# FFN up products of a decoder layer: seven half-size block products in place of eight

## The chip, the cores and the metric

The kernel is one launch on one core of a Trainium2 chip. The metric is the device time of one execution in microseconds (us); lower is better. TensorE (PE; PEld is its weight load), VectorE (DVE), ScalarE (ACT), GpSimd (POOL) and SyncE (SP, which issues most loads) each work through their own instruction list in order, and wait for each other through semaphores.

## The reference, cut to what matters

A decoder layer runs on 512 prompt rows and on 32 sample rows (8 sequences of 4), so on 544 rows of width 1024: a mixer of mLSTM and differential attention, cross attention into memory, and at the end a convolutional FFN. Only this last part and the norm ahead of it are touched:

```python
h = rms_norm(x, g_ffn_pre)
u = h @ w_up                                   # 1024 -> 2 * 2752
ext = jnp.concatenate([conv_buf, u], axis=1)
c = b_dw
for j in range(CONV_W):                        # width 3, causal, per feature
    c = c + ext[:, j:j + T] * w_dw[j]
a, g = c[..., :D_FF], c[..., D_FF:]
y = (jax.nn.silu(g) * a) @ w_down              # 2752 -> 1024
x = x + rms_norm(y, g_ffn_post)
```

The first 2752 columns of `w_up` give values, the last 2752 gates. Results must hold float32 accuracy.

## The kernel before, in words

**Accuracy.** Each float32 operand is kept as two tiles, a rounded "hi" part and a "lo" rest (`split`: ACT casts hi, L142; DVE, or POOL where it is named, subtracts to get lo, L143). A product is three matmuls: hi by hi, hi by lo, lo by hi.

**Weights.** `W` is a list of loads in the order of use. There are four slots for split weights. A slot's next content is split when the slot is freed, and its load waits in one of six stage buffers of 1024 columns.

**Rows.** The projection before the FFN (`proj_add`) works in blocks of 128 rows, sample rows first. Its `second` half adds the residual (`ev1`, L1067), and TensorE transposes each block (`norm_turn`, L317) into `fT`: features on partitions, 544 rows on the free axis, in two tiles `q` of four 128-feature steps `k`. The FFN norm's factor for each row is not applied there. `rows_of` computes it (L1079), a small matmul spreads it over all partitions (`spread`, L1459 and L1460), and the up evacuation multiplies by it.

**Up.** The 2752 features are 21 tiles of 128 and a last one of 64, whose value and gate share one tile: 43 up tiles. For each, `gemmB` (L452) runs 8 steps k by 3 matmuls by 2 halves of the rows (256 and 288 columns): 48 matmuls. `Up.ev` takes both halves from PSUM with the row factor (L1486 to L1490) into `u`, and applies the convolution with three DVE operations (L1495 to L1497) into `c`. `gate` takes the silu on ACT (L1503), multiplies on DVE (L1509), and splits the product into `act`. The first four up tiles run half by half (L440), so that they can start before the last row blocks are transposed.

**Groups.** Value and gate of one feature tile are a pair. Pairs go in groups of four; the group [20, 21] stands third. The up products of a group and of the first pair of the next come before the down products of the group (L1584 to L1586, with the sample rows in L366), which are added to `yp` (L1597).

**Order.** The code is written in this order, and the framework's scheduler then fixes one list for each engine. Nothing is reordered at run time.

Of the kernel before, what the change touches and what calls it, by code (L numbers as in the profile page):

```python
# [41 lines left out]
HALF = ((0, 256), (256, ROWS))  # L42

# [30 lines left out]
def kernel(ctx: ExitStack, tc: tile.TileContext, I, O):  # L74
# [15 lines left out]
    npool = ctx.enter_context(tc.tile_pool(name="npool", bufs=5))  # L90
# [94 lines left out]
    warm = cst.tile([P, 512], BF16, name="warm")  # L185
# [93 lines left out]

    def put(xt, q, j0, j1, c0, n, src, eng=None):  # L280
# [29 lines left out]
    def norm_turn(h, n, gname, xt, c0, pool=(True, False)):  # L310

        tmps = []
        for q in range(2):
            ps = at("tp")
            pv = v2(ps, P)[:, :, :n]
            for j in range(4):
                tr(pv[:, j, :], h[:, (4 * q + j) * P:(4 * q + j + 1) * P], ident[:n, :n])  # L317
            tmp = T2([P, 4, n], "ht")
# [10 lines left out]
    class Fill:  # L329
# [5 lines left out]
        def add(self, *gens):  # L335
            self.q.extend(gens)
# [94 lines left out]
    def gemmB(xt, evacs, half_first=False):  # L431

        if half_first:
            slots = [W.get() for _ in evacs]
            for i, (c0, c1) in enumerate(HALF):
# [10 lines left out]
        for ev in evacs:  # L446
# [11 lines left out]
            yield 1.36  # L458

# [505 lines left out]
    csz = cst.tile([P, NB, NS], F32, name="csz")  # L965
# [62 lines left out]
    def proj_add(xt, gname, src, gname2, dst, order=None, scale=None):  # L1028
# [44 lines left out]
        def rows_of(x, n, c0):  # L1073
            if scale is None:
                pend.append((norm_rows(x, n, ACTROWS), n, gname2, target[0], c0, POOLQ))
                return
            pend.append((x, n, gname2, target[0], c0, POOLQ))
            rs = sm.tile([P, 1], F32, name="rsd", tag="rsd", bufs=5)
            VCP(out=rs[:n], in_=rstd(sumsq(x, n, N("hN")[:n]), n, 1, DM))  # L1079
            scale[1].append((rs[:n], c0, n))  # L1080
# [349 lines left out]
    groups = [list(range(g, g + 4)) for g in range(0, 20, 4)]  # L1430
    groups.insert(2, [20, 21])

    def up_slots(js):
        for j in js:
            if j < 21:
# [14 lines left out]
    fT = XT("fT")  # L1450

    rsb = cst.tile([P, ROWS], F32, name="rsb")
    rss = []

    def spread(i):
        while rss and (i or len(rss) > 2):
            rs, c0, n = rss.pop(0)
            ps = at("rsb")
            mm(ps[:, :n], lhsT=rs.broadcast_to([n, P]), rhs=ident[:n, :n], start=True, stop=True)  # L1459
            VCP(out=rsb[:, c0:c0 + n], in_=ps[:, :n])  # L1460

    proj, second = proj_add(oT, "g_mem_post", lambda b: xd[0][rows(b)[0]:rows(b)[0] + rows(b)[1], :], "g_ffn_pre", xd[1],
                            scale=(rsb, rss))
# [8 lines left out]
    class Up:  # L1472


        def __init__(self, ti, cvo):
            self.ti, self.cvo = ti, cvo
# [264 lines left out]
```

## Time and profile before

| | |
|---|---|
| median of 3 runs | 1006.27 us (1004.79 to 1007.79) |
| the profiled execution's own time | 1007.98 us |
| its span | 1006.2 us |
| TensorE busy | 983.6 us (98%) |
| DVE, ACT, POOL busy | 601.6, 386.4, 196.9 us |
| mean granted TensorE clock | 0.989 |
| up matmuls in groups (L452 on fT) | 1872 |

The FFN fills the span from about 587 us on. A row of a group has busy time and mean duration of one behind the first bar, and the engine's idle time ahead of it behind the second. Matmuls are pipelined, so that a record is longer than the distance to the next one; the distance is what counts. The windows view gives each engine's busy time in a stretch.

### The profile page before, as it was taken

How to read it: one execution, taken by the hardware profiler on the slowest of the kernel's cores; microseconds unless marked ns; L12 is line 12 of the kernel's file. 1: busy time of each engine (PE TensorE's matmuls, PEld its weight loads, DVE VectorE, ACT ScalarE, POOL GpSimd, SP SyncE). 2: the span in 40 equal slices, each digit the busy share in tenths (PEclk: the TensorE clock that was granted, in tenths of full speed). 3: DMA queues.
4: the chain of work that ended last, by engine and by line, in shares of the span. 5: the costliest groups of instructions: out<-in, count | busy, mean ns of one | idle time of the engine just before them, and what ended most of it. 6: DMA issues, size and time to landing. Idle time of an engine off the chain costs nothing.

```text
span 1006.2 us, 17149 instructions
## 1 busy us (share of the span) xinstructions
PE 983.6 (98%) x6666; PEld 824.3 (82%) x6666; DVE 601.6 (60%) x1127; ACT 386.4 (38%) x740; POOL 196.9 (20%) x389
## 2 busy tenths in 40 slices
PE   8999999999999999999999999999999999999994
PEld 5999777789765778898667789979987997997983
DVE  6834225642686456743654587836857685675677
ACT  6743322333176547633542443242222222222232
POOL 6610000112232114500000164401101110110115
PEclk9999999999899999999999999999999999999998
DMA  9940224151544267763861673053132314214113
GB/s 305 300 128 22 68 79 129 49 175 35 166 138 128 67 209 229 268 214 130 314 220 38 214 236 106 25 147 84 43 118 67 103 46 126 86 44 131 38 46 110
DMA packets 120402, 130.28 MB, mean 129 GB/s; under 512 B 8423, under 2 KB 85832, under 8 KB 120320
## 3 DMA queue, kind: packets, MB, share of 16 engines
q1 hardware_dynamic: 114136, 125.69, 39.7%
q10 hardware_dynamic: 6184, 3.48, 1.2%
q8 instruction: 53, 0.87, 0.3%
q14 instruction: 29, 0.24, 0.1%
HBM read 112.22 MB, written 16.93 MB: 128 GB/s over the span
## 4 chain that ended last, share of the span: by engine, by line
PE 90%; DMA 3%; DVE 3%; issue 1%; ACT 1%; POOL 1%; SPq 0%; DVEq 0%; POOLq 0%; ACTq 0%
PE mm L452 31%; PE mm L386 7%; PE mm L388 7%; PE mm L387 7%; PE mm L440 6%; PE mm L1584 4%; PE mm L1586 4%; PE mm L1585 4%; PE mm L366 3%; PE sda L1137 2%; PE tpk L1342 1%; PE sca L1293 1%; PE cpo L1323 1%; PE ssc L1352 1%; PE oda L1163 1%
## 5 line engine op out<-in xcount | busy, mean ns | idle before, releaser
L142 ACT CAST wslot<-wst 128x1024 fp32r<-128x1024 f32 (+1 forms) x127 | 131.1, 1036 | 282.0 <-issue 82.5
L452 PE MATMUL mm<-fT,wslot 128*128 128x256 f32 (+1 forms) x1872 | 235.7, 288 | 0.0
L452 PEld LDWEIGHTS mm<-fT,wslot 128*128 128x128 f32 x1872 | 234.7, 188 | 0.7 <-issue 0.4
L143 DVE TENSOR_TENSOR wslot<-wst,wslot 128x1024 fp32r<-128x1024 f32 (+1 forms) x127 | 154.0, 1215 | 117.1 <-ACT wslot L142 117.0
L1584 PE MATMUL mm<-wslot,act 128*128 128x512 f32 (+1 forms) x176 | 70.7, 409 | 0.0
L1585 PE MATMUL mm<-wslot,act 128*128 128x512 f32 (+1 forms) x176 | 69.5, 395 | 0.0
L1586 PE MATMUL mm<-wslot,act 128*128 128x512 f32 (+1 forms) x176 | 69.0, 397 | 0.0
L1491 POOL COPY cvo<-u 128x2 f32<-128x2 f32 x43 | 16.2, 377 | 222.4 <-DVE u L1489 222.4
L386 PE MATMUL mm<-wslot,hT 128*128 128x512 f32 x128 | 52.5, 413 | 0.0
L387 PE MATMUL mm<-wslot,hT 128*128 128x512 f32 x128 | 51.8, 405 | 0.0
L452 PE MATMUL mm<-hT,wslot 128*128 128x288 f32 (+1 forms) x384 | 51.4, 295 | 0.0
L388 PE MATMUL mm<-wslot,hT 128*128 128x512 f32 x128 | 51.1, 402 | 0.0
L452 PEld LDWEIGHTS mm<-hT,wslot 128*128 128x128 f32 x384 | 50.0, 194 | 0.1
L1584 PEld LDWEIGHTS mm<-wslot,act 128*128 128x128 f32 (+1 forms) x176 | 33.1, 189 | 17.7 <-issue 8.6
L1486 DVE TENSOR_TENSOR u<-mm,rsb 128x256 f32<-128x256 f32 x43 | 18.1, 423 | 43.6 <-PE mm L452 43.5
L1586 PEld LDWEIGHTS mm<-wslot,act 128*128 128x128 f32 (+1 forms) x176 | 33.0, 188 | 7.5
L1585 PEld LDWEIGHTS mm<-wslot,act 128*128 128x128 f32 (+1 forms) x176 | 33.1, 188 | 6.5
L1503 ACT ACTIVATE c<-c 128x560 f32<-128x560 f32 x21 | 14.1, 673 | 57.3 <-DVE c L1497 53.8
L1497 DVE SCALAR_TENSOR_TENSOR c<-u,cvT,c 128x560 f32<-128x560 f32 x43 | 34.3, 797 | 0.8
L1496 DVE SCALAR_TENSOR_TENSOR c<-u,cvT,c 128x560 f32<-128x560 f32 x43 | 34.1, 793 | 0.1
L386 PEld LDWEIGHTS mm<-wslot,hT 128*128 128x128 f32 x128 | 24.4, 190 | 10.5 <-issue 5.8
L1597 DVE TENSOR_TENSOR yp<-mm,yp 128x512 f32<-128x512 f32 x40 | 27.3, 689 | 9.5 <-PE mm L1586 9.4
(444 smaller groups left out, 1900.9 us busy)
## 6 DMA issues: line engine op xcount, KB each, us to landing
wst<-in_w_up_dram SPq DMA_DIRECT2D x42, 512.0 KB
wst<-in_w_in_dram SPq DMA_DIRECT2D x28, 512.0 KB
wst<-in_w_down_dram SPq DMA_DIRECT2D x20, 512.0 KB
wst<-in_cache_mem_k_dram SPq DMA_DIRECT2D x16, 512.0 KB
vt<-in_cache_mem_v_dram SPq DMA_DIRECT2D x8, 1024.0 KB
wst<-in_w_mk_dram SPq DMA_DIRECT2D x8, 512.0 KB
xb<-in_x_prompt_dram SPq DMA_DIRECT2D x8, 512.0 KB
wst<-in_cache_dk_dram SPq DMA_DIRECT2D x16, 256.0 KB
```

Source lines behind the costliest of these rows:

```text
L142: nc.scalar.copy(out=hi, in_=src)
L143: (eng or nc.vector).tensor_tensor(out=lo, in0=src, in1=f32(hi), op=SUB)
L386: mm(ps[b], lhsT=xt.hi(k, c0, c0 + n), rhs=s[:, 0, kk, :], start=(k == 0), stop=False)
L387: mm(ps[b], lhsT=xt.hi(k, c0, c0 + n), rhs=s[:, 1, kk, :], start=False, stop=False)
L388: mm(ps[b], lhsT=xt.lo(k, c0, c0 + n), rhs=s[:, 0, kk, :], start=False, stop=(k == nk - 1))
L440: mm(ps, lhsT=s[:, l, k, :], rhs=x(k, c0, c1), start=(k == 0 and j == 0), stop=(k == 7 and j == 2))
L452: mm(ps[i], lhsT=s[:, l, k, :], rhs=x(k, c0, c1), start=(k == 0 and j == 0), stop=(k == 7 and j == 2))
L1496: STT(out=c, in0=u[:, 1:EXT - 1], scalar=w[1], in1=c, op0=MUL, op1=ADD)
L1497: STT(out=c, in0=u[:, 0:EXT - 2], scalar=w[0], in1=c, op0=MUL, op1=ADD)
L1584: mm(ps, lhsT=t[:, 0, c0:c0 + P], rhs=s[:n, 0, i % 2, :], start=st, stop=False)
L1585: mm(ps, lhsT=t[:, 0, c0:c0 + P], rhs=s[:n, 1, i % 2, :], start=False, stop=False)
L1586: mm(ps, lhsT=t[:, 1, c0:c0 + P], rhs=s[:n, 0, i % 2, :], start=False, stop=en)
```

## The change

The 20 full pairs no longer run as two up tiles of 8 steps by 2 halves each. A pair's weights are cut into 2 by 2 blocks (value or gate, first or last 512 features), and the rows into two halves of 272 columns (256 prompt rows and 16 sample rows each). Eight block products of 12 matmuls become seven (Winograd's form of Strassen's scheme), each of 4 steps k by 3 matmuls on 272 columns. The sums that this needs are made in float32 and then split:

- of the rows, once (`Sevenths.sums`): three sums on POOL and one on DVE of 1088 columns each, four splits;
- of the weights, for each pair (`slotsS`): four sums of 512 columns on POOL, in place in the stage buffers, and four slots per pair: the value tile as loaded (`own`), one gate block (`other`, half a slot), and the two tiles after the sums (`sums`);
- of the products (`run`): some accumulate in one PSUM bank; four intermediate results (`p1`, `p4`, `p5`, `u2`) are copied from PSUM by ACT, and four additions on DVE take one bank and one copy into `u`.

Sums over rows need rows that are normed already, so the norm is applied before the transposes (`norm_rows`: sum of squares, factor, ACT multiply), and the factor at the evacuation is gone. `fT` is also kept in float32 (`XE.full`). The convolution's first step goes from DVE to ACT. The tiles 20 and 21, which stay on `gemmB`, come first. The stretch of code that matters:

```diff
+    def slotsS(w, ca, cb):
...
+        def other():
+            sv = tile_of()
+            (a1, a2), (b1, b2) = ((t[:, 0:4], t[:, 4:8]) for t in st)
+            split(sv[:, 0, 0:4], sv[:, 1, 0:4], b2)
+            GTT(out=b2, in0=b1, in1=b2, op=ADD)
+            GTT(out=b1, in0=a1, in1=b1, op=SUB)
+            GTT(out=a1, in0=b2, in1=a1, op=SUB)
+            GTT(out=a2, in0=a2, in1=a1, op=SUB)
+            return sv
...
+        for emit in (own, other, sums(0), sums(1)):
+            W.add(emit)
+
+    class Sevenths:
...
+        def sums(self):
+
+            (x11, x12), (x21, x22) = ((t[:, :, :HR], t[:, :, HR:]) for t in self.xt.full)
+            GTT(out=x11, in0=x12, in1=x11, op=SUB)
+            VTT(out=x12, in0=x22, in1=x12, op=SUB)
+            GTT(out=x22, in0=x22, in1=x11, op=SUB)
+            GTT(out=x21, in0=x21, in1=x22, op=SUB)
+            self.t3 = x12
+            for name, t in (("t4", x21), ("t1", x11), ("t2", x22)):
+                o = self.op[name] = [npool.tile([P, 4, HR], F32R, name="xo", tag="N") for _ in range(2)]
+                split(*o, t)
...
+        def run(self, ua, ub):
...
+            pa, pd, pe, pc = (mmp()[:, :HR] for _ in range(4))
+            s = W.get()
+            self.product(pa, s, 0, ("x", 0, 0))
+            p1 = keep(pa, "p1")
+            self.product(pd, s, 1, ("x", 1, 0))
+            W.free()
+            add(ua, 0, pd, p1)
+            s = W.get()
+            self.product(pe, s, 0, "t4")
+            W.free()
+            p4 = keep(pe, "p4")
+            s, s2 = W.get(), W.get()
+            self.product(pc, s2, 1, "t1")
+            p5 = keep(pc, "p5")
+            self.product(pa, s, 0, "t2", False)
+            u2 = keep(pa, "u2")
+            self.product(pc, s, 1, ("x", 1, 1), False)
+            W.free()
+            add(ua, 1, pc, u2)
+            ua.end()
+            self.product(pa, s2, 0, "t3", False)
+            W.free()
+            add(ub, 1, pa, p5)
+            add(ub, 0, pa, p4)
+            ub.end()
...
         def rows_of(x, n, c0):
-            if scale is None:
-                pend.append((norm_rows(x, n, ACTROWS), n, gname2, target[0], c0, POOLQ))
-                return
...
+            pend.append((norm_rows(x, n, ACTROWS), n, gname2, target[0], c0, POOLQ))
...
-    groups = [list(range(g, g + 4)) for g in range(0, 20, 4)]
-    groups.insert(2, [20, 21])
+    groups = [[20, 21]] + [list(range(g, g + 4)) for g in range(0, 20, 4)]
...
-                VTT(out=u[:, 2:258], in0=ps, in1=rsb[:, 0:256], op=MUL)
...
-            VTS(out=c, in0=u[:, 2:EXT], scalar1=w[2], scalar2=cvT[:, ti, 19:20], op0=MUL, op1=ADD)
+            ACT(out=c, in_=u[:, 2:EXT], func=AF.Identity, scale=w[2], bias=cvT[:, ti, 19:20])
```

In the three places below the number behind a name tells one use of a tile from another.

**TensorE, from one pair to the next within a group.** Before, an up tile's matmuls go through one slot in order, alternating between the two halves of the rows:

```order
L452 MATMUL mm_7294<-fT00_6092,wslot_7142 128x256
L452 MATMUL mm_7295<-fT00_6092,wslot_7142 128x288
L452 MATMUL mm_7294<-fT10_6093,wslot_7142 128x256
L452 MATMUL mm_7295<-fT10_6093,wslot_7142 128x288
L452 MATMUL mm_7294<-fT00_6092,wslot_7142 128x256
```

Now (mm_7731 is the bank `pa` of one pair, mm_7881 and mm_7884 are `pa` and `pc` of the next, wslot_7834 and wslot_7857 the next pair's two summed weight tiles; xo_6420 and xo_6421 are hi and lo of `t2`, xo_6416 and xo_6417 those of `t1`):

```order
L556 MATMUL mm_7731<-fT10_6090,wslot_7707 128x272
L556 MATMUL mm_7731<-fT00_6089,wslot_7707 128x272
L556 MATMUL mm_7881<-xo_6420,wslot_7834 128x272
L556 MATMUL mm_7881<-xo_6421,wslot_7834 128x272
L556 MATMUL mm_7884<-xo_6416,wslot_7857 128x272
L556 MATMUL mm_7884<-xo_6417,wslot_7857 128x272
L556 MATMUL mm_7881<-xo_6420,wslot_7834 128x272 x2
L556 MATMUL mm_7881<-xo_6421,wslot_7834 128x272
```

The next pair's first three products stand ahead of this place already. The last product of one pair (`t3`) is followed at once by products on the next pair's two summed weight tiles.

**DVE at the same place.** Before, the evacuation of one up tile, its convolution, and the lo part of one weight slot:

```order
L1486 TENSOR_TENSOR u_7349<-mm_7294,rsb_5811 128x256
L1489 TENSOR_TENSOR u_7349<-mm_7295,rsb_5811 128x256
L1490 TENSOR_TENSOR u_7349<-mm_7295,rsb_5811 128x8x4
L1495 TENSOR_SCALAR c_7357<-u_7349,cvT_5765 128x560
L143 TENSOR_TENSOR wslot_7345<-wst_7344,wslot_7345 128x1024
L1496 SCALAR_TENSOR_TENSOR c_7357<-u_7349,cvT_5765,c_7357 128x560
L1497 SCALAR_TENSOR_TENSOR c_7357<-u_7349,cvT_5765,c_7357 128x560
```

Now (L567 is the addition of a bank and a copy, L145 the lo subtraction of `split`):

```order
L567 TENSOR_TENSOR u_7860<-mm_7731,p5_7806 128x256
L567 TENSOR_TENSOR u_7860<-mm_7731,p5_7806 128x4x4
L567 TENSOR_TENSOR u_7860<-mm_7731,p4_7792 128x256
L567 TENSOR_TENSOR u_7860<-mm_7731,p4_7792 128x4x4
L1619 SCALAR_TENSOR_TENSOR c_7841<-u_7768,cvT_5765,c_7841 128x560
L145 TENSOR_TENSOR wslot_7834<-wst_7761,wslot_7834 128x1024
L145 TENSOR_TENSOR wslot_7857<-wst_7763,wslot_7857 128x1024
L145 TENSOR_TENSOR wslot_7915<-wst_7911,wslot_7915 128x1024
L145 TENSOR_TENSOR wslot_7935<-wst_7913,wslot_7935 128x512
L1618 SCALAR_TENSOR_TENSOR c_7869<-u_7860,cvT_5765,c_7869 128x560
L1619 SCALAR_TENSOR_TENSOR c_7869<-u_7860,cvT_5765,c_7869 128x560
```

The lo parts of the next pair's summed weights (wslot_7834, wslot_7857) now stand behind both additions that read the bank of this pair's last product (mm_7731).

**POOL where the FFN begins.** Before, the lo parts of the last row block's transposes are followed by small copies of conv rows:

```order
L143 TENSOR_TENSOR fT10_6093<-ht_6418,fT00_6092 128x4x128
L143 TENSOR_TENSOR fT11_6105<-ht_6427,fT01_6104 128x4x128
L1491 COPY cvo_6298<-u_6333 128x2
L1492 COPY cvo_6298<-u_6333 128x16
L1491 COPY cvo_6298<-u_6380 128x2
L1492 COPY cvo_6298<-u_6380 128x16
```

Now the sums of the rows (L538, L540, L541 on fTf, the float32 form of fT) and of the first pair's weights (L509 to L512 on wst):

```order
L538 TENSOR_TENSOR fTf_5810<-fTf_5810 128x4x272
L145 TENSOR_TENSOR fT10_6090<-fTf_5810,fT00_6089 128x4x128
L145 TENSOR_TENSOR fT11_6100<-fTf_5811,fT01_6099 128x4x128
L540 TENSOR_TENSOR fTf_5811<-fTf_5811,fTf_5810 128x4x272
L509 TENSOR_TENSOR wst_6257<-wst_6257 128x512
L541 TENSOR_TENSOR fTf_5811<-fTf_5811 128x4x272
L510 TENSOR_TENSOR wst_6257<-wst_6255,wst_6257 128x512
L1613 COPY cvo_6285<-u_6311 128x2
L1614 COPY cvo_6285<-u_6311 128x16
L1613 COPY cvo_6285<-u_6357 128x2
L1614 COPY cvo_6285<-u_6357 128x16
L511 TENSOR_TENSOR wst_6255<-wst_6257,wst_6255 128x512
```

Where POOL had the last two lo parts and small copies, there is now one queue of long sums with these lo parts inside it, behind the first sum.

More of the change, by code (lines that the diff above doesn't have):

```diff
@@ L1448 @@
         up_slots(nxt[1:])
[L1450 to L1463, printed above, removed]
+    fT = XE("fT")
+    proj, second = proj_add(oT, "g_mem_post", lambda b: xd[0][rows(b)[0]:rows(b)[0] + rows(b)[1], :], "g_ffn_pre", xd[1])
     run(proj)
     pend = second(fT)
-    yp = [S([P, 2, DM], F32, "yp") for _ in range(2)]
+    yp = []
     ys = cst.tile([P, 2, 256], F32, name="ys", tag="xs")
```

117 lines of the change are left out of this document (90 added, 27 removed).

## The prediction

> **What bounds the kernel now.** I read the busy totals and the chain of waits, then the FFN by windows (columns: length, then PE, PEld, DVE, ACT and POOL busy with counts, granted clock, DMA share, GB/s), then its waits (total us, times, longest).
>
> ```profile
> PE 983.6 (98%) x6666; PEld 824.3 (82%) x6666; DVE 601.6 (60%) x1127; ACT 386.4 (38%) x740; POOL 196.9 (20%) x389
> PE 90%; DMA 3%; DVE 3%; issue 1%; ACT 1%; POOL 1%; SPq 0%; DVEq 0%; POOLq 0%; ACTq 0%
> ...
> 616.20:652.60 36.40, 36.40 (x293) 36.33 (x291) 32.63 (x60) 12.59 (x15) 15.56 (x29) 1.00 0.23 65
> 652.60:676.60 24.00, 24.00 (x126) 18.02 (x125) 9.37 (x13) 9.21 (x14) 0.71 (x5) 1.00 0.47 132
> 676.60:724.60 48.00, 48.00 (x383) 47.78 (x382) 34.07 (x61) 13.52 (x17) 6.05 (x31) 1.00 0.24 68
> ...
> DVE u L1486 <- PE mm L452: 43.5, 33, 3.9
> ```
>
> In an up stretch of four pairs (48 us) and in the down stretch ahead of it (24 us) TensorE is busy from end to end at clock 1.00, and DVE waits for it. So the FFN costs what its matmuls cost as long as the others keep up. The nearest behind is DVE: 34.07 of 48, and 32.63 of 36.4 at the start.
>
> **Removed: 240 matmuls.** A full pair had 2 tiles of 48, so 96, and has 7 products of 12, so 84; twelve times 20 pairs is 240. Their distance (start, us, engine, line):
>
> ```profile
> 931.53 35.94 PE mm L452 x288
> ...
> 593.69 4.86 PEld L440 LDWEIGHTS mm<-fT,wslot 128*128 128x128 f32 x40
> ...
> 604.03 12.28 PEld L440 LDWEIGHTS mm<-fT,wslot 128*128 128x128 f32 x92 [0.80 <-POOL fT L143]
> ...
> L452 PE MATMUL mm<-fT,wslot 128*128 128x288 f32 x923 | 222.4, 294 | 0.0
> ```
>
> Alternating halves of 256 and 288 columns stand 35.94/288 = 0.125 us apart. One bank at a time, as a product runs, they stand about (4.86 - 0.19)/39 = 0.120 us apart for 256 columns and (12.28 - 0.19)/91 = 0.133 us for 288, so 0.126 for 272. A pair falls from 96 x 0.125 = 12.0 us to 84 x 0.125 or 0.126, 10.5 to 10.6 us. Over 20 pairs that is 27 to 30 us; I take **-28.5**. Tiles 20 and 21 keep their 144 matmuls. The loads are the same in bytes, and the removed row-factor matmuls and copies count as nothing, since they fell into gaps.
>
> **Added on DVE and ACT for each pair.** These are the rows of an up tile (683.64 on) and the groups of the FFN (x count, busy, mean ns of one, idle before):
>
> ```profile
> 683.64 0.42 DVE L1486 TENSOR_TENSOR u<-mm,rsb 128x256 f32<-128x256 f32 x1 [3.53 <-PE mm L452]
> 683.99 0.41 DVE L1489 TENSOR_TENSOR u<-mm,rsb 128x256 f32<-128x256 f32 x1
> 684.32 0.18 DVE L1490 TENSOR_TENSOR u<-mm,rsb 128x32 f32<-128x32 f32 x1
> 684.61 0.57 DVE L1495 TENSOR_SCALAR c<-u,cvT 128x560 f32<-128x560 f32 x1
> 685.09 1.22 DVE L143 TENSOR_TENSOR wslot<-wst,wslot 128x1024 fp32r<-128x1024 f32 x1
> 686.23 0.79 DVE L1496 SCALAR_TENSOR_TENSOR c<-u,cvT,c 128x560 f32<-128x560 f32 x1
> 687.06 0.80 DVE L1497 SCALAR_TENSOR_TENSOR c<-u,cvT,c 128x560 f32<-128x560 f32 x1
> ...
> L142 ACT CAST wslot<-wst 128x1024 fp32r<-128x1024 f32 x55 | 57.8, 1051 | 178.3 <-issue 65.0 <-PE mm L452 60.7 <-PE mm L1586 50.3
> L143 DVE TENSOR_TENSOR act<-a,act 128x544 fp32r<-128x544 f32 x21 | 15.1, 718 | 3.6 <-ACT act L142 3.6
> L1509 DVE TENSOR_TENSOR a<-c 128x512 f32<-128x512 f32 x21 | 14.5, 691 | 11.2 <-ACT c L1503 11.2
> L1503 ACT ACTIVATE c<-c 128x560 f32<-128x560 f32 x21 | 14.1, 673 | 57.3 <-DVE c L1497 53.8 <-DVE cvr L1552 3.4
> L142 ACT CAST act<-a 128x544 fp32r<-128x544 f32 x21 | 13.5, 643 | 7.4 <-DVE a L1513 7.4
> L143 DVE TENSOR_TENSOR wslot<-wst,wslot 128x512 fp32r<-128x512 f32 x2 | 1.4, 693 | 0.0
> L1595 ACT COPY ys<-mm 128x256 f32<-128x256 f32 x2 | 0.7, 373 | 3.1 <-PE mm L366 3.1
> L1513 DVE TENSOR_TENSOR a<-c 128x32 f32<-128x32 f32 x21 | 3.9, 185 | 0.0
> ```
>
> ACT gets 3.5 casts where it had 2, four copies and two first convolution steps: 3.5 x 1.05 + 4 x 0.4 (0.37 for 256 columns of PSUM, here 272) + 3 x 0.67 + 0.64 = 7.9 us. That fits under 10.5. DVE, by distances between starts, has three lo subtractions of 1.14, half a one of 0.69, four additions of 0.34 with their short pieces of at most 0.18, four convolution steps of 0.83, the gate at 0.69 + 0.19 and its lo part at 0.72: 3.4 + 0.7 + 2.1 + 3.3 + 0.9 + 0.7 = **11.1 us against 10.5 of matmuls**. It was 2.3 + 1.7 + 1.1 + 3.3 + 0.9 + 0.7 = 10.0 against 12.0. So the cover is gone: within a group DVE is the bound, and what stands where in its list counts.
>
> **The new wait, between two pairs.** After `t3` of one pair TensorE's list goes on with six matmuls (0.75 us), and then with the lo part of the next pair's summed weights. In DVE's list that lo part stands behind the two additions that read `t3`'s bank and one convolution step. From the start of the last matmul's successor: the result comes 0.294 - 0.125 = 0.17 us later, the additions take 1.05, the step 0.83, the subtraction 1.22, in sum 3.3; less 0.75 leaves 2.5 us idle. Nothing can fill it, since TensorE's list is fixed. Bounds: 1.9 if the short pieces and the hop cost nothing and the subtraction frees the matmuls at its distance instead of its end, 3.5 if the cast ahead of the subtraction is late by one turn of 1.0 us because POOL's last sum is (next paragraph). I take 2.8, nearer to 2.5, which rows make up. It happens before the third and the fourth pair of each of the five groups of four: 10 x 2.8 = **+28** (19 to 35). A group's second pair follows down products and has its splits done beside them. A group's first pair, which stands ahead of the down products, waits for the same subtraction without the convolution step (2.4), with two matmuls and some sample matmuls between, and then about 0.6 for the next subtraction: 4 x 2.0 = **+8** (2 to 12), the first group's being counted under the FFN's beginning.
>
> **POOL.** Four sums of 512 columns per pair. POOL's own row, and a stretch where POOL and DVE both work on two SBUF inputs of 512 columns:
>
> ```profile
> 602.70 2.53 POOL L143 TENSOR_TENSOR fT<-ht,fT 128x512 fp32r<-128x512 f32 x2 [0.41 <-ACT fT L142]
> ...
> 13.26 6.87 POOL L219 TENSOR_TENSOR wslot<-wst,wslot 128x512 fp32r<-128x512 f32 x4
> ...
> 15.49 5.18 DVE L219 TENSOR_TENSOR wslot<-wst,wslot 128x512 fp32r<-128x512 f32 x3
> ```
>
> Alone a sum is 1.27 us, so 5.1 a pair, within 10.5. Together each needs 1.72, and DVE's 0.69 becomes 1.73 too: they take turns. In DVE's pauses for ACT (silu, act cast) POOL gets its turn for nothing; otherwise the chain of sums is late, and with it the ACT cast, behind which ACT's copies from PSUM are queued. This is the 3.5 above, and the second rival.
>
> **Where the FFN begins.** Norming the rows puts the ACT multiply behind the factor, and the first sum stands in POOL's list ahead of the last block's lo parts. Chain of waits there:
>
> ```profile
> 583.04 0.87 PE tp L317 x8
> ...
> 586.04 0.68 DVE ht L319
> ...
> 597.88 0.75 DVE xb L1067
> ...
> 598.79 1.16 ACT hN L298 x2
> ...
> 600.03 0.20 POOL rs L292
> ...
> 600.31 0.55 POOL rs L293
> ```
>
> The last block's rows are done at 598.6 and their factor at 600.9, as before. The multiply (the sum of squares' 1.06 without its read, about as long) gives 601.9, the first four transposes 602.4, the DVE multiply and the hop 603.3. Then POOL: a sum of 1088 columns, 1.27 x 1088/512 = 2.7 us, and a lo part, 1.27: 607.3. TensorE fills with 24 hoisted matmuls until about 606. Its 69 matmuls end near 616; `t4` needs L540, L509 and L541 in POOL's list (608.5 + 2.7 + 1.3 + 2.7 = 615.2) and a split of 2.4: 617.6. `t2` needs three more weight sums with the small copies between (5.0), a cast and a subtraction (2.3): 622.5. By then 180 matmuls are done, where before 192 were at 616.3: behind by 6.2 + 1.5, about **+8** (5 with pauses that overlap, 11 with turns against DVE).
>
> **Sum.** 1007.98 (the profiled execution: 1006.2 of span and 1.8 around it) - 28.5 + 28 + 8 + 8 = 1023.5. That execution lies 1.7 above the median of the runs, so a median near **1022**. All low ends give 1004 - 1.7, all high ends 1039 - 1.7.
>
> **Rivals.** (1) The others keep up, and the time falls. For it: DVE idled 14 of 48 us, the splits of a group's second pair fall into the down stretch, and the up products run half a pair ahead. If a place between pairs costs 1.0 instead of 2.8, the boundary 0.5 and the beginning 5: 1007.98 - 28.5 + 10 + 2 + 5 - 1.7 = 995; with no waits at all between pairs 983. Against it: the three operations ahead of the subtraction are in DVE's list, whatever its load. (2) The turns decide: each of the four sums holds DVE for 1.72 - 0.69 = 1.03 us more, DVE then needs 15.2 us a pair, 4.7 above the matmuls, at ten places, with boundaries at 3 and the beginning at 11: 1007.98 - 28.5 + 47 + 12 + 11 - 1.7 = 1048. For it: the shared turns at 13 to 21 us. Against it: DVE has pauses there. The Trainium skill's page "SBUF — State Buffer" (section "Who interferes with whom") states that a DVE operation with two SBUF inputs and a GpSimd one that reads SBUF block each other for the whole instruction; by that a sum would hold DVE 1.27, and the same sum gives 1058. The turns in the trace agree with the rule, their length less. (3) The gain and the waits cancel: 1.6 us a place, 1 a boundary, 7 at the beginning, 1005. That the matmuls aren't saved can't be: the list has 84 a pair, and 0.126 bounds their distance.
>
> **Chances.** Forecast (1009 to 1040) 0.58, first rival (983 to 1003) 0.23, the third 0.12, the second 0.07. The likeliest's own range is 1009 to 1036; to leave out no more than 2 in 10 I take 998 to 1036, which reaches halfway into the first rival's cases. 0.3% is about what can be told from no change: faster 0.23, within it 0.12, slower 0.65.
>
> **What would show it.** Right: L556 x1680 at 0.125 us; in the waits, PE or PEld on L556 behind DVE's weight lo part (L145) and ACT's cast about 14 times for 2 us or more; DVE near full in the up stretches; some 8 us of idle TensorE between 600 and 625; sums on L509 to L512 at 1.3 to 1.8 us. Wrong: up windows in which PE stays busy from end to end and four pairs take under 43 us, or waits that name POOL or PSUM copies instead.

## The result: slower by 6%, with time lost at the FFN's beginning and in every group

The changed kernel takes 1069.75 us (median of 5 runs, 1064.16 to 1071.52) against 1007.79 (median of 5 runs, 1004.79 to 1011.89). The ratio is 1.0606, 95% interval [1.0574, 1.0637]. The prediction had the direction, but 1022 and a range that ended at 1036.

The page of the changed kernel (the span, the busy totals, and the TensorE clock granted in 40 slices, in tenths):

```profile
span 1062.4 us, 17013 instructions
...
PE 985.8 (93%) x6416; PEld 812.6 (76%) x6416; DVE 641.3 (60%) x1148; ACT 486.8 (46%) x924; POOL 331.3 (31%) x472
...
PEclk9999999999899999999999887999999989989997
```

TensorE has 250 matmuls fewer, and yet 56 us more pass. Its clock falls in the slices where the FFN begins (23 to 25), and again in two groups.

In the profiles of all runs the FFN starts up to 12 us earlier or later (580 to 592), for reasons that lie ahead of the change. So the stages are compared by their own length: from the last matmul of the projection, which both kernels have, to the end of the span. That matmul in the timeline of TensorE (start, us, engine, line), first of before, then of the changed kernel:

```profile
585.61 0.40 PE L388 MATMUL mm<-wslot,oT 128*128 128x512 f32 x1
```

```profile
583.43 0.40 PE L417 MATMUL mm<-wslot,oT 128*128 128x512 f32 x1
```

So the FFN takes 1006.2 - 585.6 = **420.6 us** before and 1062.4 - 583.4 = **479.0 us** after, 58.4 more. The windows show where. Each but the first and the last goes from the end of one group's down products to the end of the next's (length, then PE, PEld, DVE, ACT and POOL busy, clock, DMA share, GB/s). Before, its first window and a middle one:

```profile
585.60:677.30 91.70, 89.94 (x637) 82.30 (x636) 65.26 (x113) 33.63 (x47) 33.08 (x61) 1.00 0.41 124
...
784.70:858.00 73.30, 73.30 (x516) 66.81 (x515) 49.23 (x84) 17.57 (x20) 7.03 (x36) 1.00 0.30 85
```

The changed kernel, all six; the first ends with the down products of tiles 20 and 21:

```profile
583.40:662.30 78.90, 57.30 (x318) 45.19 (x317) 51.34 (x61) 41.13 (x71) 45.85 (x51) 0.83 0.28 83
662.30:742.20 79.90, 73.50 (x467) 64.50 (x466) 55.26 (x90) 35.41 (x53) 33.48 (x52) 0.96 0.26 74
742.20:820.50 78.30, 71.83 (x468) 63.26 (x467) 56.95 (x93) 34.94 (x52) 33.43 (x52) 0.98 0.29 82
820.50:898.90 78.40, 72.64 (x467) 64.30 (x466) 57.27 (x94) 34.74 (x52) 35.78 (x52) 0.96 0.28 82
898.90:981.70 82.80, 74.42 (x468) 65.40 (x467) 57.44 (x92) 34.74 (x52) 32.14 (x52) 0.94 0.27 78
981.70:1049.00 67.30, 60.63 (x383) 52.24 (x382) 50.19 (x90) 32.22 (x58) 26.92 (x43) 0.97 0.19 67
```

A group of four pairs took 73.3 us with TensorE busy throughout. It has 48 matmuls fewer now, and without gaps it would take some 73.3 - 5.6 = 67.7. It takes 78.3 to 82.8. In the first window TensorE is idle for 21.6 of 78.9 us.

**The beginning** in the timeline of TensorE (in brackets the idle time ahead, and what ended it):

```profile
584.55 1.09 PE L343 MATMUL tp<-cpk,hN 128*128 128x128 f32 x8 [0.73 <-ACT hN L331]
591.96 1.05 PE L469 MATMUL mm<-fT,wslot 128*128 128x272 f32 x3 [6.32 <-ACT fT L144]
...
620.89 0.39 PE L556 MATMUL mm<-xo,wslot 128*128 128x272 f32 x1 [1.23 <-ACT xo L144]
628.38 0.41 PE L1682 MATMUL cvo<-cpk,cvo 128*54 128x128 f32 x1 [7.09 <-POOL cvo L1614]
...
653.43 0.80 PE L1711 MATMUL mm<-wslot,act 128*128 128x512 f32 x1 [2.63 <-ACT yp L1722]
```

Three gaps stand out: 6.3 us between the second block's transposes and the first up products, 7.1 us inside the first `t4` product, and 2.6 us in the down products of the short group. In the second, TensorE's list has a transpose of the convolution rows (L1682) behind the first matmul of `t4`. It needs POOL's last small copy, which stands behind a sum in POOL's list:

```profile
624.69 2.31 POOL L511 TENSOR_TENSOR wst<-wst 128x512 f32<-128x512 f32 x1
...
628.13 0.19 POOL L1614 COPY cvo<-u 128x16 f32<-128x16 f32 x1
```

Without the row sums (run 4) this gap is 1.5 us.

**A place between two pairs** in the middle group, TensorE, then DVE, ACT and POOL in fences of their own:

```profile
771.16 0.52 PE L556 MATMUL mm<-xo,wslot 128*128 128x272 f32 x2 [1.41 <-ACT wslot L144]
772.10 0.52 PE L556 MATMUL mm<-xo,wslot 128*128 128x272 f32 x2 [0.43 <-ACT wslot L144]
773.35 1.52 PE L556 MATMUL mm<-xo,wslot 128*128 128x272 f32 x10 [0.73 <-DVE wslot L145]
```

```profile
771.37 0.79 DVE L1619 SCALAR_TENSOR_TENSOR c<-u,cvT,c 128x560 f32<-128x560 f32 x1
772.08 4.09 DVE L145 TENSOR_TENSOR wslot<-wst,wslot 128x1024 fp32r<-128x1024 f32 x4
```

```profile
769.30 0.36 ACT L563 COPY p<-mm 128x272 f32<-128x272 f32 x1
770.06 3.46 ACT L144 CAST wslot<-wst 128x1024 fp32r<-128x1024 f32 x4 [0.39 <-POOL wst L512]
```

```profile
762.40 1.80 POOL L509 TENSOR_TENSOR wst<-wst 128x512 f32<-128x512 f32 x1 [4.73 <-DVE wslot L145]
...
768.74 1.28 POOL L512 TENSOR_TENSOR wst<-wst 128x512 f32<-128x512 f32 x1
```

TensorE waits 2.6 us here, about the 2.8 that was forecast. The first cast ends near 771.1, and DVE, which has additions and a convolution step first, takes up the lo parts at 772.1: about 1 us of the wait is DVE's list, the rest lies ahead of the casts. Read backwards: they start at 770.06, when POOL's last sum is done (768.74 + 1.28 = 770.02). POOL's first sum started at 762.40, when the gate block's lo part was done, because the sum overwrites that block in its stage buffer. So four sums and the small copies between them take 7.6 us of the 14 that a pair takes (1.0 of it POOL waits for one of DVE's additions), and casts and subtractions follow only then. That is one reading; the runs test it. The rows leave a second: ACT's own list holds it until 769.66 with a convolution step and a copy, so it waits for POOL for 0.39 us only. At the next place of this group it doesn't wait at all: the casts start at 783.57, right behind a convolution step, and POOL's last sum ended at 783.53.

### The profile page after: what moved, and what is told of

It is laid out like the page before. It is cut to its first block, busy times and chain, and to the rows that moved or that the text cites. A ratio compares the mean times of both kernels' runs of the same rounds, so it can differ in the third digit from the quotient of the medians.

```text
span 1062.4 us, 17013 instructions
## 1 busy us (share of the span) xinstructions
PE 985.8 (93%) x6416; PEld 812.6 (76%) x6416; DVE 641.3 (60%) x1148; ACT 486.8 (46%) x924; POOL 331.3 (31%) x472
## 4 chain that ended last, share of the span: by engine, by line
PE 66%; DVE 15%; DMA 5%; issue 5%; POOL 4%; ACT 3%; SPq 1%; DVEq 0%; POOLq 0%; ACTq 0%
PE mm L556 9%; PE mm L481 7%; PE mm L415 6%; PE mm L416 5%; PE mm L417 5%; PE mm L469 5%; DVE wslot L145 4%; PE mm L1711 3%; PE mm L1712 3%; PE mm L1713 3%; PE mm L395 3%; PE sda L1266 2%; DVE c L1618 2%; DVE c L1619 2%; DVE u L567 2%
## 5 line engine op out<-in xcount | busy, mean ns | idle before, releaser
L145 DVE TENSOR_TENSOR wslot<-wst,wslot 128x1024 fp32r<-128x1024 f32 (+1 forms) x167 | 189.0, 1151 | 112.1 <-ACT wslot L144 111.7
L144 ACT CAST wslot<-wst 128x1024 fp32r<-128x1024 f32 (+1 forms) x167 | 160.5, 985 | 176.8 <-PE mm L1713 53.2
L556 PE MATMUL mm<-fT,wslot 128*128 128x272 f32 x960 | 133.4, 293 | 4.9 <-ACT p L563 4.3
L556 PE MATMUL mm<-xo,wslot 128*128 128x272 f32 x720 | 114.1, 311 | 25.5 <-ACT wslot L144 12.8
L556 PEld LDWEIGHTS mm<-fT,wslot 128*128 128x128 f32 x960 | 127.3, 192 | 10.0 <-ACT p L563 6.4
L556 PEld LDWEIGHTS mm<-xo,wslot 128*128 128x128 f32 x720 | 102.9, 205 | 34.0 <-ACT wslot L144 16.3
L509 POOL TENSOR_TENSOR wst<-wst 128x512 f32<-128x512 f32 x20 | 30.7, 1534 | 105.4 <-DVE wslot L145 105.4
L1617 ACT ACTIVATE c<-u,cvT 128x560 f32<-128x560 f32 x43 | 36.8, 856 | 34.2 <-DVE u L567 32.3
L1711 PEld LDWEIGHTS mm<-wslot,act 128*128 128x128 f32 (+1 forms) x176 | 34.5, 196 | 22.8 <-issue 6.5
L1713 PEld LDWEIGHTS mm<-wslot,act 128*128 128x128 f32 (+1 forms) x176 | 34.0, 193 | 7.7
L567 DVE TENSOR_TENSOR u<-mm,p 128x256 f32<-128x256 f32 x120 | 28.7, 291 | 18.4 <-PE mm L556 18.3
```

What stands on the lines that cost most here:

```text
L144: nc.scalar.copy(out=hi, in_=src)
L145: (eng or nc.vector).tensor_tensor(out=lo, in0=src, in1=f32(hi), op=SUB)
L556: mm(ps, lhsT=s[:, l, 4 * e + k, :], rhs=x[m][:, k, :], start=first and k + j == 0, stop=(k == 3 and j == 2), skip_group_check=True)
L1711: mm(ps, lhsT=t[:, 0, c0:c0 + P], rhs=s[:n, 0, i % 2, :], start=st, stop=False)
L1713: mm(ps, lhsT=t[:, 1, c0:c0 + P], rhs=s[:n, 0, i % 2, :], start=False, stop=en)
```

## The experiments

Each run's figure is the length of its FFN as defined above, from its own profile; before has 420.6, the changed kernel 479.0. Behind it stands the time of the run. Each kernel has one profile, so how far an FFN's length varies from one execution to the next was not measured. A group in which TensorE never waits agrees within 0.2 us between kernels (73.3 to 73.5), but whole times of one kernel differ by up to 12 us (ten executions of run 12: 1000.70 to 1012.87). Differences of 2 or 3 us between two single runs are therefore weak.

**1. All pairs without block products, norm and order as changed**

```diff
+    SEVEN = ()
...
-            if gi:
+            if gi and j in SEVEN:
                 seven[0].run(*tiles[i])
+            elif gi:
+                run(gemmB(fT, [t.ev for t in tiles[i]], halves=EVEN))
```

> All 20 pairs run as two tiles of eight steps again, with no sums of rows or weights; rows normed beforehand, tiles 20 and 21 first, evacuation and first convolution step on ACT stay as in the changed kernel. Theory (the lost time is: some 24 us of idle TensorE at the FFN's beginning, some 42 in the groups, some 17 of halved clock; of the beginning only the wait of 6.5 us at 585 belongs to the norm): the 28 us of matmuls come back, the groups run without gaps, the clock stays near 0.99, and the time is 1010 to 1020. Rival 1 (the norm and the new order cost nothing, all of the beginning belongs to the sums): 1000 to 1010. Rival 2 (most of the beginning belongs to norm and order): over 1025.

441.5 us (1027.87). Rival 2 holds: 20.9 of the 58.4 us have nothing to do with the seven products. Its first two windows:

```profile
584.50:655.00 70.50, 58.49 (x331) 47.11 (x330) 34.86 (x46) 37.08 (x69) 28.30 (x41) 0.82 0.41 120
655.00:730.80 75.80, 75.80 (x515) 69.12 (x514) 38.68 (x51) 30.15 (x61) 17.11 (x36) 0.97 0.29 82
```

Later groups take 73.4 us as before. So the beginning costs 20.9 without sums, and sums add 78.9 - 70.5 = 8.4.

**2. The weight sums left out**

```diff
-            GTT(out=b2, in0=b1, in1=b2, op=ADD)
-            GTT(out=b1, in0=a1, in1=b1, op=SUB)
-            GTT(out=a1, in0=b2, in1=a1, op=SUB)
-            GTT(out=a2, in0=a2, in1=a1, op=SUB)
```

> The four sums of weights on POOL are left out, so the products use unsummed weights; all else stays. Theory (a pair of 14.5 us in the groups is DVE's: 11.1 of its own work, 1.4 by which operations last longer beside POOL's sums, 2 of waits for ACT): ten places get 1.4 shorter and the beginning 4, so 1046 to 1056, with pairs of about 13 us and DVE operations back at their old lengths. Rival 1 (POOL's chain of four sums sets when the splits can start, and so the period): the gaps between pairs go, 1020 to 1035. Rival 2 (POOL is off the path): 1064 to 1070.

448.6 us (1036.29), 30.4 less: the edge of rival 1, and 10 below the theory's range. A group takes 72.8 to 75.0, still 5 or more above 67.7.

**3. The weight sums on DVE**

```diff
-            GTT(out=b2, in0=b1, in1=b2, op=ADD)
+            VTT(out=b2, in0=b1, in1=b2, op=ADD)
...
```

> The four sums of weights go from POOL to DVE, 4 x 0.61 to 0.69 us a pair. Theory (DVE's list is the bound): 2.4 to 2.8 more and 1.4 less a pair, at ten places and some boundaries, 1074 to 1088. Rival 1 (POOL's chain is the bound): four sums of 0.65 in place of 1.3 to 1.8 each, so the gaps shrink by half, 1035 to 1055. Rival 2 (both cancel): 1064 to 1073.

465.5 us (1055.49), 13.5 less, where the theory had expected more time; it is at the edge of rival 1. One group of this kernel, and one of run 2 and of run 6 below, where DVE has other loads:

```profile
822.30:897.10 74.80, 69.15 (x468) 61.61 (x467) 61.89 (x109) 34.82 (x52) 14.54 (x36) 1.00 0.29 86
```

```profile
732.80:805.60 72.80, 69.42 (x468) 61.79 (x467) 51.72 (x93) 34.79 (x52) 14.49 (x36) 1.00 0.31 88
```

```profile
833.90:915.70 81.80, 72.61 (x467) 64.89 (x466) 62.13 (x102) 29.21 (x44) 36.35 (x52) 0.94 0.28 79
```

The third number behind the length is DVE's. With 61.9 us of DVE work a group takes 74.8, with 62.1 it takes 81.8, and the changed kernel takes 78.3 with 57.0. **DVE's total doesn't set the period.** What the two runs 2 and 3 share is that POOL's 7.6 us of sums are gone, and with them the longer DVE operations beside them; the scheduler also makes new lists in each run. On DVE four sums take 4 x 0.69 = 2.8, by the second of these groups (of the changed kernel, then of run 3):

```profile
L510 POOL TENSOR_TENSOR wst<-wst 128x512 f32<-128x512 f32 x12 | 18.7, 1559 | 0.9
...
L145 DVE TENSOR_TENSOR act<-a,act 128x544 fp32r<-128x544 f32 x12 | 15.0, 1249 | 7.3 <-ACT act L144 7.3
```

```profile
L510 DVE TENSOR_TENSOR wst<-wst 128x512 f32<-128x512 f32 x13 | 8.9, 687 | 0.2
...
L145 DVE TENSOR_TENSOR act<-a,act 128x544 fp32r<-128x544 f32 x12 | 8.6, 719 | 1.8 <-ACT act L144 1.8
```

**4. The row sums left out**

```diff
-            GTT(out=x11, in0=x12, in1=x11, op=SUB)
...
-                split(*o, t)
+                self.op[name] = self.op["x", q, i]
```

> The sums of rows and their splits are left out; the products take plain halves of the rows in place of the summed ones. Weights are summed as before. Theory (the row sums on POOL and their splits on DVE hold up the first pairs): of the 16.5 us of idle TensorE between 616 and 663 some 10 go, and some 5 of halved clock after them, so 1050 to 1060. Rival (the weight sums and the small copies in POOL's list hold them up anyway): 1064 to 1070.

468.5 us (1050.91), 10.5 less. The first window falls by 7.5 to 71.4 us. So the theory holds in direction, at less than the 15 that it gave.

**5. Without block products, in the old order of groups**

```diff
-    groups = [[20, 21]] + [list(range(g, g + 4)) for g in range(0, 20, 4)]
+    groups = [list(range(g, g + 4)) for g in range(0, 20, 4)]
+    groups.insert(2, [20, 21])
...
```

> As the run with all 20 pairs as two tiles of eight steps and rows normed beforehand, which took 1027.9 beside 1010.9 of the kernel before, but with the groups in the old order, tiles 20 and 21 third. Theory (norming ahead of the transposes costs the wait of 6.5 us at the first up product, some 3 in two smaller ones, and 2 to 3 of halved clock; the rest of the 17 is the short group standing first, whose down products wait and run at half clock): 10 to 12 above the kernel before, 1018 to 1023. Rival 1 (all 17 from the norm): 1025 to 1030. Rival 2 (all from the order): 1008 to 1013.

428.0 us (1010.07): 13.5 of run 1's 20.9 belong to the short group standing first, and 7.4 remain, where the theory had 10 to 12. (By the whole time it would seem 3.6, which is rival 2's number; this execution's FFN started 5 us earlier than that of before.) The first window still has a gap like the first one above:

```profile
580.30:678.60 98.30, 90.41 (x635) 83.32 (x634) 52.76 (x67) 53.65 (x103) 36.57 (x62) 0.95 0.41 121
...
581.06 1.09 PE L343 MATMUL tp<-cpk,hN 128*128 128x128 f32 x8 [0.38 <-ACT hN L331]
588.73 1.27 PE L469 MATMUL mm<-fT,wslot 128*128 128x272 f32 x4 [6.57 <-ACT fT L144]
```

**6. The first convolution step back on DVE**

```diff
-            ACT(out=c, in_=u[:, 2:EXT], func=AF.Identity, scale=w[2], bias=cvT[:, ti, 19:20])
+            VTS(out=c, in0=u[:, 2:EXT], scalar1=w[2], scalar2=cvT[:, ti, 19:20], op0=MUL, op1=ADD)
```

> The changed kernel with one thing back: the first convolution step runs on DVE again instead of ACT. Theory (DVE's list waits 0.7 to 1.0 us at each tile for ACT's step, and ACT's casts queue behind it; the step on DVE is 0.57, by distance 0.5): the hop is dearer than the work, so 0.5 to 1 us a pair less, 1055 to 1066. Rival (the sum of DVE's work sets the pair): 1.0 more a pair, 1076 to 1092. No difference: 1066 to 1072.

502.3 us (1085.81), 23.3 more: the theory fell, the rival's number came. But its reason, that DVE's total counts, is what run 3 contradicts. What the runs allow to say is that the step on DVE cost 23.3/43 = 0.54 us each, somewhat less than the 0.67 that it lasts there, and that the move to ACT was worth its price.

**7 and 8. Block products for some pairs only**

```diff
+    SEVEN = (4, 5, 8, 9, 12, 13, 16, 17)    # run 7;  run 8: (5, 9, 13, 17)
...
-            if j < 20:
+            if j in SEVEN:
                 slotsS(w_up, P * j, DFF + P * j)
```

> Seven block products only for pairs 4, 5, 8, 9, 12, 13, 16 and 17 (the first two of four groups), all other pairs as two tiles of eight steps; groups in the old order; rows normed beforehand; the row sums stand behind the first group's up products. Matmuls fall by 8 x 1.4 = 11 us. Theory (a group's second pair has its sums and splits beside the down products of 24 us, its first pair has not and waits some 3 us): equal to the same kernel without seven-product pairs, within 4 us. Rival 1 (with one such pair at a time everything keeps up): 9 to 12 us less than that kernel, near the time before. Rival 2 (the sums on POOL hold up both): 5 or more above that kernel.

> The same with seven block products only for pairs 5, 9, 13 and 17 (the second of four groups). Matmuls fall by 4 x 1.4 = 5.7 us. Theory (this pair's sums and splits lie beside down products, in which DVE and POOL are nearly idle): 4 to 6 us less than the same kernel without seven-product pairs. Rival (its sums and copies disturb the pairs around it as much): no difference or more.

429.5 (1016.2) and 425.0 us (1018.48), against 428.0 of run 5. Run 7 came as its theory said, run 8 gained 3.0 where 4 to 6 were expected. The groups show why. One group of run 7, with two such pairs, and of run 8, with one:

```profile
869.10:940.60 71.50, 71.50 (x491) 64.55 (x490) 48.40 (x73) 32.72 (x56) 23.33 (x44) 1.00 0.32 90
```

```profile
692.80:764.70 71.90, 71.90 (x503) 65.62 (x502) 42.53 (x61) 32.44 (x60) 13.33 (x36) 1.00 0.37 102
```

TensorE is busy throughout, the clock is 1.00, and a group takes 1.4 to 1.8 us less than 73.3. Up to two pairs of four cost no wait that the rows show, even with the sums on POOL. One pair gives all of its 1.4 us; two give 1.4 to 1.8 of 2.8, and where the other 1 us goes no row shows. What the runs lose, they lose in their first windows, where the row sums stand: 106.9 and 101.1 against 98.3.

**9. A buffer of its own for the transposed convolution outputs.** In the waits of the middle group of the changed kernel (engine, line, releaser: total us, times, longest) stands one that the reading above doesn't have:

```profile
PE mm L556 <- ACT wslot L144: 3.2, 3, 1.4
...
PE mm L556 <- ACT p L563: 1.5, 2, 1.2
...
ACT p L563 <- DMA out_dram<-cvr: 4.1, 2, 2.2
```

ACT's copy of a saved product waits for an output transfer. The three buffers `Z` hold both the saved products and `cvr`, the transposed convolution outputs, until their transfer has landed.

```diff
-                t = Z("cvr")[:72, :P]
+                t = T2([72, P], "cvr")
```

> The changed kernel with one thing different: the buffer that holds the transposed convolution outputs until their output transfer has landed is no longer one of the three buffers that also hold the four saved products of a pair. Theory (the saved products wait for that transfer, 18.6 us of ACT's idle time in 8 places, and TensorE then waits for ACT's copies, 0.5 to 3.4 us at a group's end): 6 to 10 us less than the changed kernel, 1059 to 1064. Rival (another wait of the same place takes over): 1066 to 1072.

469.4 us (1059.44), 9.5 less, as the theory said. A group takes 76.1 to 77.5.

**10 and 11. The old order with 18 pairs; and the same with the edits of runs 3 and 9**

```diff
-    groups = [[20, 21]] + [list(range(g, g + 4)) for g in range(0, 20, 4)]
+    SEVEN = [j for j in range(2, 20)]
+    groups = [list(range(g, g + 4)) for g in range(0, 20, 4)]
+    groups.insert(2, [20, 21])
...
-            o = self.op["t3"] = self.op["x", 0, 1]
+            t = S([P, 2, 4, HR], F32R, "t3")
+            o = self.op["t3"] = [t[:, 0], t[:, 1]]
```

(Runs 7, 8, 12 and 14 have these lines too, with their own pairs: tiles that follow as eight-step products still need the rows that `t3` would overwrite.)

> The changed kernel in the old order of groups (tiles 20 and 21 third): pairs 0 and 1 as two tiles of eight steps at the beginning, the other 18 pairs as seven block products. Theory (the short group standing first costs 13.5, as the two runs without block products showed: 1027.9 with it first, 1010.1 with it third, from different starts of the FFN): 13 less for the order, 3 more for two pairs with more matmuls, 1055 to 1063. Rival 1 (with block products the order matters no more, because the row sums hold up the first pair in any case): 1067 to 1075. Rival 2 (the row sums are hidden as well): 1045 to 1054.

> As the run in the old order with 18 pairs, and both other findings in it: the weight sums on DVE and the separate buffer for the transposed convolution outputs. Theory (the parts add up: 4 us a group for the sums, 1 to 2 for the buffer): 22 to 28 less than that run without them, 1030 to 1040, still above the kernel before, since a group of four pairs then takes 73 to 75 us against 73.2. Rival (taken together they meet another bound, DVE's own list): less than 15 us gained, 1042 to 1055. Rival 2 (all gaps between pairs close, a group takes 68 to 70): 1005 to 1020.

470.9 (1060.61) and 443.7 us (1029.3). The order gives back 8.1 net. The other two parts give 27.2 together, where singly they gave 13.5 + 9.5 = 23.0: they add up. The 27.2 lie in the theory's range of 22 to 28; the whole time is just below its 1030. With all four pairs as block products a group now takes

```profile
874.50:947.00 72.50, 69.14 (x467) 61.53 (x466) 61.31 (x109) 34.68 (x52) 12.79 (x36) 1.00 0.31 89
```

so 0.8 less than before, of the 5.6 that the matmuls would give.

**12. Three pairs of four in three groups**, with the old order, the weight sums on DVE, the buffer, and the row sums on DVE in pieces of 272 columns beside the first group's last pair

```diff
+    SEVEN = [j for j in range(8, 20) if j % 4 < 3]
...
-            GTT(out=x11, in0=x12, in1=x11, op=SUB)
...
+            for k in range(4):
+                a, b, c, d = (t[:, k] for t in (x11, x12, x21, x22))
+                VTT(out=a, in0=b, in1=a, op=SUB)
...
```

> Block products only for the first three pairs of the groups 8 to 11, 12 to 15 and 16 to 19, nine pairs; the others as two tiles of eight steps; old order of groups; row sums on DVE in small pieces beside the first group's last pair; weight sums on DVE; separate buffer for the convolution outputs. Matmuls fall by 9 x 1.4 = 12.6 us, the norm ahead of the transposes costs some 6. Theory (such pairs cost waits only where several follow one another without down products between; here one place in each group): 1000 to 1008, near the kernel before. Rival 1 (no waits at all): 996 to 1001. Rival 2 (waits as in the changed kernel): 1010 to 1020.

421.2 us; 1006.36 us (median of 10 runs), ratio to before 0.9993, interval [0.9965, 1.0021]: no difference.

**13. Run 5 without the row factor**

```diff
-            pend.append((norm_rows(x, n, ACTROWS), n, gname2, target[0], c0, POOLQ))
+            h = x if gname2 == "g_ffn_pre" else norm_rows(x, n, ACTROWS)
+            pend.append((h, n, gname2, target[0], c0, POOLQ))
```

> As the run with all pairs as two tiles of eight steps and the groups in the old order, but the row factor of the FFN norm (sum of squares, factor, ACT multiply) is left out, so rows go into the transposes as they are. From the last projection matmul to the end that run took 428.0 us, the kernel before 420.6. Theory (the 7.4 are the chain of norm ahead of the transposes: 1.25 for the sum of squares, 0.7 to 2 for the factor, 1.15 for the multiply, and what DVE puts ahead of the late transposes' multiply): 420 to 423. Rival (the equal row halves, which need 16 sample rows for the first product, and the evacuation on ACT): 425 to 428.

418.0 us (999.81): 10.0 less than run 5, more than the theory's 5 to 8, and 2.6 less than before. The gap ahead of the first up products is gone:

```profile
580.27 1.03 PE L343 MATMUL tp<-cpk,xb 128*128 128x128 f32 x8
581.06 0.98 PE L469 MATMUL mm<-fT,wslot 128*128 128x272 f32 x4
```

So the norm ahead of the transposes costs 10.0 against no factor at all. The other new parts (equal halves, evacuation on ACT, no row factor there) would be worth 2.6; that is one difference of single runs, and this kernel also lacks the factor's own work, which before has beside its products.

**14. Run 12 with pairs 5 and 6 as well**

```diff
-    SEVEN = [j for j in range(8, 20) if j % 4 < 3]
+    SEVEN = [j for j in range(5, 20) if j % 4 < 3]
```

> As the run with nine pairs as block products, which measured 0.9993 of the time before, with pairs 5 and 6 added, eleven in all. Theory (a group with block products takes 70.2 to 70.7 instead of 73.2; the row sums are done beside the first group's last pair and its down products, so that pair 5 doesn't wait): 2 to 3 us less, 1002 to 1005, about 0.997. Rival (the row sums and their splits hold up pair 5): equal or slower, 1006 to 1012.

417.3 us; 1001.75 us (median of 10 runs, 999.03 to 1009.06), ratio 0.9963, interval [0.9932, 0.9993]. So it is 0.4% faster than before, just clear of no difference. Its last full groups take 70.7 and 70.1 us:

```profile
782.20:852.90 70.70, 69.90 (x480) 62.95 (x479) 57.95 (x98) 34.72 (x56) 10.76 (x37) 1.00 0.32 91
852.90:923.00 70.10, 69.57 (x479) 62.96 (x478) 56.07 (x95) 33.67 (x54) 9.73 (x36) 1.00 0.33 92
```

## Why the prediction was wrong

The 58.4 us, by differences of runs: norm ahead of the transposes +10.0 (runs 5 and 13), equal halves and evacuation on ACT -2.6 (run 13 and before), short group first +13.5 (runs 1 and 5), block products +37.5 (run 1 and the changed kernel). In the last, the matmuls gave -28; weight sums on POOL cost 30.4 (run 2), row sums 10.5 (run 4), the shared buffer 9.5 (run 9). If these add, as runs 10 and 11 suggest for two of them, some 15 are left that no run took apart. The forecast's terms come to 15.5: of the 43 us that it lacked, 21 lie at the FFN's beginning and 21 in the groups.

- **What bounds the kernel before: right.** Run 5 shows it again, with DVE busy for 39 us of a group instead of 49 and the same 73.3.
- **Matmuls removed, -28.5: right.** In the changed kernel's timeline 24 of them take 3.18 us (742.48 on), so (3.18 - 0.29)/23 = 0.126 apart.
- **DVE at 11.1 us a pair is the bound of a group: wrong.** This is the first step that failed. The sum was fair: 4 x 11.1 and the 9.4 of the down products are 53.8, and run 2, without POOL's sums beside it, has 51.7. But in runs 3 and 6 equal totals on DVE go with periods of 74.8 and 81.8.
- **The new wait between two pairs, 2.8 us at ten places: size near, releaser wrong.** In the middle group the two places have 2.6 and 2.5 us (1.41 + 0.43 + 0.73, and 1.31 + 1.18), and some 0.9 more behind DVE's additions. Only 0.73 of the first is behind DVE's lo part; 1.84 is behind ACT's casts, and the second place waits for ACT alone. Those casts start when POOL's last sum has ended and ACT's own list has reached them, which is within 0.4 us of each other. Without POOL's sums (run 2) both places of a group have one wait of 0.8 us between them, behind an ACT copy; there the scheduler also puts the splits further ahead in DVE's list. So the sums on POOL are shown to cost this time, but whether by the length of their chain or by the place that the casts and splits then get in the lists of ACT and DVE stays open. The prediction had the chain of sums in view, but priced it as one turn of 1.0 us in an upper bound, and didn't follow it back to its start: four sums in a row that can't begin before the gate block is split. That the size came out near is luck as far as the releaser is another.
- **Group boundaries, 2.0 us each: cause missed.** The saved products share three buffers with the outputs (run 9). In the timeline the four boundaries wait 0.3 to 3.3 us behind ACT's copies, 6.0 in all against the 8 of the sum.
- **Places and boundaries together: 36 forecast, some 57 found, but not all of it waits.** The 57 are 86.4, which beginning and groups lost (58.4 + 28), less the 29.3 of the beginning. By the five windows from 662.3 on, TensorE is idle for 33.7 us, and 3.9 of that is a wait in the last group behind POOL's copies `acs` (L1638), which had no term. So places and boundaries have some 30, below the forecast. Matmuls at half clock, which had no term either, cost some 9 more there (last section). The rest, some 14, isn't taken apart; part of it are pauses shorter than a matmul's record, which don't count as idle.
- **The FFN's beginning, +8: as large a miss, 29.3 found** (10.0 - 2.6 + 13.5 + 8.4). The prediction followed the norm's chain for the last row block alone. The first up products need the second block, and there the sum of squares, the factor and the multiply now stand ahead of the transposes. They come late enough for DVE's list to have other work first:

```profile
586.00 3.52 DVE L1202 SCALAR_TENSOR_TENSOR xb<-y,rs,xb 128x512 f32<-128x512 f32 x2
589.45 1.21 DVE L145 TENSOR_TENSOR wslot<-wst,wslot 128x1024 fp32r<-128x1024 f32 x1
590.58 1.28 DVE L303 TENSOR_TENSOR fTf<-tp,gT 128x512 f32<-128x512 f32 x2
```

  The transposes end at 585.6, and their multiply starts at 590.6. The order of groups had no term in the sum, though the short group's down products then have less work beside them. By the sum of long matmuls that is told of below, some 4.8 of the 13.5 are half clock (6.0 us in the first two windows of run 1, 1.2 in the first of run 5). The rest is idle time around the short group's down products, for which three up tiles and one pair are all the cover; no run takes it apart further. Of the 8.4 that sums add, the longest wait is the transpose's behind POOL's small copies (7.1 us, 1.5 in run 4): the prediction had these copies in POOL's list, but not the transpose in TensorE's.
- **The rivals.** The second, with turns between POOL and DVE (1048, or 1058 by the cited rule), pointed to the right pair of engines, and had 0.07. Its mechanism was only part of it: a pair's operations on DVE get longer by 1.3 us, not 4.1 (group of four: 57.0 against 51.7 without sums). The first and the third rival fell.
- **The marks.** The sums lasted 1.29 to 1.56 us on average in the groups, inside the 1.3 to 1.8 that were named, and the matmuls' distance was right. The mark that was given for wrong came true: the waits lead to POOL and to PSUM copies.

## What to carry to other kernels

A step that is moved ahead of another must be priced where its first consumer stands, not where its last instance ends; and an order of work costs cover even if no instruction changes. An operand that is made by a chain (sum, cast, subtraction) on several engines has to be judged by the chain's length from the moment when its buffer may be written, and by where each link stands in its engine's list, against the time to its use; totals per engine don't show it. Where such a chain doesn't fit, do it for as many units as find cover: here two of four pairs showed no wait, three gave 2.9 of 4.2 us, and four at best 0.8 of 5.6, so that a kernel with eleven pairs of twenty came out 0.4% ahead of before.

## What the hardware showed that was not expected

**The clock.** The prediction's sum had no term for it. Windows of 4 us of the changed kernel (PE busy is the first number behind the length, the clock the third from the end):

```profile
584.00:588.00 4.00, 1.09 (x8) 0.85 (x8) 4.00 (x5) 4.00 (x7) 2.13 (x3) 0.92 0.47 146
588.00:592.00 4.00, 0.04 (x1) 0.04 (x1) 4.00 (x5) 1.86 (x5) 3.63 (x10) 0.50 0.80 239
...
596.00:600.00 4.00, 4.00 (x28) 4.00 (x28) 2.11 (x3) 1.33 (x3) 0.98 (x3) 0.80 0.49 192
...
648.00:652.00 4.00, 2.33 (x10) 0.97 (x6) 3.23 (x3) 1.04 (x2) 3.84 (x5) 1.00 0.49 131
652.00:656.00 4.00, 2.57 (x5) 1.66 (x6) 1.58 (x3) 3.75 (x7) 1.61 (x3) 0.52 0.00 0
656.00:660.00 4.00, 4.00 (x9) 1.92 (x8) 1.23 (x1) 1.01 (x3) 0.00 (x0) 0.50 0.27 71
```

In the gap from 585.6 to 592.0 the clock fell to half. It was back at 597.6 (0.80 from 596 to 600 is 1.6 us at half), 5.6 us after work had begun again and 3.4 after the next gap had ended at 594.2. From 652 to about 666 it was at half once more; TensorE was busy from 656 to 660 and did 9 down products, which at 0.23 us apart would be 17. Summed over all matmuls whose records are longer and which stand up to twice their usual distance apart, this costs some 13 us in the changed FFN, some 9 of it from 662 on, and in the one before none. The Trainium skill's page "TensorE: Matmul & The Clock Gate" (section "What's actually happening") states that the clock is halved after an idle window of about 3.4 us and restored after as much sustained work. The gaps of 6.3 and 7.1 us agree with that. The stretch from 652 on differs: its longest gap was 2.6 us, with TensorE busy for 2.3 of the 4 us ahead of it. Nor does it take that much: from 788.7 to 792.1 the clock was 0.50, and the two gaps ahead of it, which ended at 785.61 and 788.53, were 1.3 and 1.2 us long, with TensorE busy for 1.9 of the 3.4 us from 785.3 on.

**POOL beside DVE.** With POOL's sums running, DVE's lo part of the product lasted 1.25 us instead of 0.72 (rows at run 3), while POOL's own sums took 1.29 to 1.56 on average, where one alone takes 1.27. The Trainium skill's page "SBUF — State Buffer" (section "Who interferes with whom") calls the ports that these two engines share an exclusive lock. Here DVE bears most of it: a pair's operations on DVE get 1.3 us longer, and its four sums on POOL 0.6.
